# Hybrid encoder layer on one core: which engine makes the rest of an fp32r split for two weight units and four blocks of the down projection, an unrounded input summed instead of copied, and other banks for the keys' transposes

## Chip, cores and metric

The kernel runs on one core of a Trainium2 chip. The metric is the device time in microseconds (us) of one execution. A core has a matrix engine (TensorE, called PE in the profile), a vector engine (VectorE, DVE), a scalar engine (ScalarE, ACT), GpSimd (POOL) and a queue engine that starts DMAs (SyncE, SP). Every engine works through its own instructions in order and waits on semaphores.

## What is computed

One layer of an encoder for 512 tokens of width 1024, in float32: token mixing by two groups of heads (8 query heads over 2 key heads with a rotary embedding, and 4 heads of a two-way gated recurrence), cross attention of 4 heads into 256 memory tokens, and a gated feed-forward part of width 2816 with a convolution of three taps along the tokens. Each part has an RMS norm ahead and one behind.

```
h = rmsnorm(x, pre_mix_g)
aq, ak, av, hq, hf_fwd, hf_bwd, hi, hg = split_columns(h @ w_in, IN_SPLITS)
att = axial_gqa_attention(rope(rmsnorm(aq)), rope(rmsnorm(ak)), av)
rec = hgrn2_group(hq, hf_fwd, hf_bwd, hi, hg, lb, hg_out_norm_g)
x = x + rmsnorm(concatenate([att, rec]) @ w_out, post_mix_g)
h, m = rmsnorm(x, pre_x_g), rmsnorm(mem, mem_norm_g)
x = x + rmsnorm(memory_cross_attention(h, m, w_xq, w_xkv, w_xo), post_x_g)
h = rmsnorm(x, pre_ffn_g)
x = x + rmsnorm(conv_ffn(h, w_up, conv_w, conv_b, w_down), post_ffn_g)
```

## The kernel before

**Arithmetic.** A float32 operand is held as two fp32r parts: a high part, which is the value rounded by ACT (the cast in `split`, L118, `nc.scalar.copy(hi, src)`), and a low part, which is the rest, `src - hi` by DVE (L119). A product is three matmuls, high by high, high by low, low by high (`mm3`, L243 to L245); TensorE sums them in a bank of PSUM. PSUM has four kinds of bank, b, s, c and o, two of each.

**Weights.** They come in units of 128x1024 (512 KB), loaded by SP's queue into a raw buffer. `issue` (L198) makes the two parts three units ahead of the use (AHEAD). For most units ACT casts and DVE subtracts. For the units in NEG_SCALAR ACT casts (L212), ACT writes the negative of the high part into the low part (L214), and a DMA of GpSimd's queue adds the weight from DRAM to it once more (L217, `accum_op=ALU.add`); for those in NEG_POOL GpSimd makes the negative (L216).

**Order.** A scheduler puts the instructions of each engine in order when the program is built, out of the order of the code, the buffers that are free and its own estimates; the chip then keeps to that order on each engine. The large activations share 16 buffers ("big" in the profile).

**Keys.** While the recurrence of the last head and the attention run, `attention_filler` projects the memory's keys: eight projections, each of 24 matmuls of 128x256 into a bank b (`proj_fm`), which `put_kx` splits out of the bank by ACT and DVE. After the second and the third of them (KEY_TURNS) `turn_k` transposes the rotated keys of the token blocks 0, 1 and 2, 3 on TensorE (L715, four transposes each) into a bank b as well, and ACT copies them out (L716). L607 is a matmul of the recurrence into a bank c, between them.

**Into the feed-forward part.** `between` and `turn_in` make its input: DVE scales a block of 128 rows, TensorE transposes it into two banks (L282), and `split` takes the high part (ACT) and the low part (DVE) out of each bank. A third reader, ACT at L289, copies the unrounded values of each bank into `fulls`, two buffers of 128x4x512; there are four row blocks with two banks each, so eight copies of 128x512.

**Up projection.** 22 steps i; in five of them (5, 8, 11, 14, 17) a pair of column blocks is made by Strassen's seven products (`strassen_pair`). These need four differences of parts of the input, which `sum_of_h` makes from `fulls` (L1080, a subtraction of 128x1024 by DVE, then a split), one after each of the four units of the steps i = 2 and 3. The convolution of each step is `conv` (L1039 to L1053).

**Down projection.** Seven products p in Strassen's manner, each over three groups g of feed-forward blocks; a product takes 22 half units of weight, and two row blocks b. `left_side(p, g)` (L1010) prepares the left operand of one product and group: it splits a difference or a part of an activation into `hi` and `lo`. `lay_ahead` does this three groups ahead; (0,0) comes at the step i = 20 and (0,1), (0,2) at the end of the up projection. For most (p, g) it is ACT and DVE. For those in NEG_GROUP ACT casts (L1022), GpSimd writes the negative into `lo` (L1023), and a DMA of GpSimd's queue adds the source to it, from SBUF to SBUF (L1024). At p = 3 DVE overwrites a side buffer with another difference (L1014).

Of the kernel before, what the change touches and what calls it, by code (L numbers as in the profile page):

```python
# [9 lines left out]
F32 = mybir.dt.float32  # L10
# [8 lines left out]
P = 128  # L19
D = 1024  # L20
T = 512
# [16 lines left out]
UP_PRODUCTS = ("w11", "w22", "t2", "w21", "t1", "t3", "t4")  # L38
LAY_AHEAD, LOAD_AHEAD = 3, 5
SIDES_AT = (18, 19)  # L40
NEG_GROUP = frozenset((p, 1) for p in (1, 2, 5, 6))
AHEAD = 3
HOLD_BLOCK = 4
TURN_STEP, MEM_TURN, UP_TURN = 0, (0, 4), (0, 2)
NEG_SCALAR = frozenset(range(7, 31))
NEG_POOL = frozenset(range(31, 42))
CORE_SHARE, ATT_LEAD = 53.0, 4.0
KEY_TURNS = {1: (0, 1), 2: (2, 3)}
# [38 lines left out]
def layer(tc, io, out):  # L87
    nc = tc.nc
# [16 lines left out]
    def bank(tag):  # L105
        return ps.tile([P, 512], F32, name="ps_" + tag, tag=tag)

    def big(shape, dt=F32):
        return b8.tile(shape, dt, name="big", tag="big")
# [137 lines left out]
    def blk(b):  # L247
        return slice(b * P, (b + 1) * P)
# [26 lines left out]
        nc.vector.scalar_tensor_tensor(out=h[:, half(c)], in0=xb[:, half(c)], scalar=r, in1=g[:, half(c)],  # L275
                                       op0=ALU.mult, op1=ALU.mult)

    def turn_in(h, act, b, tags, keep=None):
        for c in range(2):
            o = bank(tags[c]).rearrange("p (k n) -> p k n", k=4)  # L280
            for k in range(4):
                nc.tensor.transpose(o[:, k, :], h[:, blk(c * 4 + k)], ident)  # L282
            hi, lo = act.hi, act.lo
            if len(hi) == 2:
                split(hi[c][:, :, blk(b)], lo[c][:, :, blk(b)], o)
            else:
                split(hi[0][:, c * 4:c * 4 + 4, blk(b)], lo[0][:, c * 4:c * 4 + 4, blk(b)], o)
            if keep:
                nc.scalar.copy(keep[c][:, :, blk(b)], o)  # L289

    def row_rstd(xb, h):
        ss = small()
# [13 lines left out]
        nc.vector.scalar_tensor_tensor(out=xb[:, cols], in0=yg, scalar=ss[:, R:R + 1], in1=xb[:, cols],  # L306
                                       op0=ALU.mult, op1=ALU.add)

    def between(x, g_post, g_pre, act, keep=None):
        def first(b, y):  # L310
            ss = small()
            return ss, residual_part(ss, y, g_post, 0, half(0), False, "th")

        def second(b, got, y):
            h = tmp4([P, D])
            ss = small()
            got = got[0], (got[1], residual_part(got[0], y, g_post, 1, half(1), True))
            for c in range(2):
                residual_add(got[0], got[1][c], x[b])
                nc.scalar.activation(h[:, half(c)], x[b][:, half(c)], ACT.Square, accum_out=ss[:, c:c + 1])  # L320
                rstd_part(ss, c, c == 1)
            for c in range(2):
                scale_rows(x[b], ss[:, R:R + 1], g_pre, h, c)
            return lambda: turn_in(h, act, b, y_tags[0][b] + y_tags[1][b], keep)
        return first, second

    def new_act():
# [37 lines left out]
    y_tags = ("b", "b", "c", "c"), ("s", "s", "o", "o")  # L365
# [68 lines left out]
    hT = new_act()  # L434
# [274 lines left out]
                                in1=kd[:, :, 0].bitcast(F32), op=ALU.subtract)  # L709

    def turn_k(b):
        o = bank("b").rearrange("p (k n) -> p k n", k=4)
        kd4 = qkv["kd"][:, b].rearrange("p a b c d -> p (a b) (c d)")
        for i in range(4):
            nc.tensor.transpose(o[:, i, :].bitcast(F32R), kd4[:, i, :], ident_r)  # L715
        nc.scalar.copy(qkv["kT"][:, :, blk(b)], o)  # L716
# [27 lines left out]
    tm_tags = ("s", "s", "o", "o")  # L744

    kv = {}
# [157 lines left out]
    x = load_x()  # L904
    g_post, g_pre = gains("post_mix_g", "pre_x_g")
    hT = new_act()

    turns = res_second(mix, MIX_ORDER, kv["y0"], between(x, g_post, g_pre, hT))
# [5 lines left out]
    qx, ox = Act([None] * 4, [None] * 4), Act([None] * 4, [None] * 4)  # L914
# [65 lines left out]

    g_post, g_pre = gains("post_x_g", "pre_ffn_g")
    hT = new_act()
    fulls = [big([P, 4, T]) for _ in range(2)]
    turns = res_second(ox, range(4), kv["x0"], between(x, g_post, g_pre, hT, fulls))

    acts, sides, gates, last_act = [], [], {}, [None]
    half_t = [slice(0, 256), slice(256, 512)]
# [75 lines left out]
    for part in range(2):  # L1063
        cols = slice(part * 256, part * 256 + 256)
        for n in range(4):
            for kc in range(8):
                mm3(us[n][:, cols], (ws[n][0][:, kc, :], ws[n][1][:, kc, :]), hT.get(kc, cols), kc == 0, kc == 7)
            if part:
                conv(*first[n], us[n])
            elif n in UP_TURN:  # L1070
                turns.popleft()()
    wide = [big([P, 2, 4, 256]) for _ in range(2)]
    s1, s2, s3, s4 = wide[0][:, 0], wide[0][:, 1], wide[1][:, 0], wide[1][:, 1]
    (a11, a21), (a12, a22) = [[f[:, :, t] for t in half_t] for f in fulls]
    sums_of_h = [(t[:, 0], t[:, 1]) for t in (big([P, 2, 4, 256], F32R) for _ in range(4))]
    of_h = [(s1, a21, a22), (s2, a11, s1), (s3, a21, a11), (s4, a12, s2)]

    def sum_of_h(k):
        o, i0, i1 = of_h[k]
        nc.vector.tensor_sub(o, i0, i1)  # L1080
        split(*sums_of_h[k], o)
# [43 lines left out]
    for i in range(2, NF):  # L1125
        if i in UP_S:
            strassen_pair(i)
        else:
            for c in range(2):
                o = next_bank()  # L1130
                w = unit(8)
                for kc in range(8):
                    mm3(o, (w[0][:, kc, :], w[1][:, kc, :]), hT.get(kc, slice(0, T)), kc == 0, kc == 7)
                conv(c, i, o)
                if i < 4:
                    sum_of_h(2 * i - 4 + c)
        if i % 3 == 2 and i // 3 < 6:
            new_sums(i // 3)

# [173 lines left out]
```

## Time and profile before

| | us |
|---|---|
| median of 3 runs | 825.16 (824.77 to 825.99) |
| the profiled execution | 825.72 |
| its span, first to last instruction | 823.8 |
| TensorE busy | 808.1 (98%) |
| VectorE busy | 568.5 (69%) |
| ScalarE busy | 473.0 (57%) |
| GpSimd busy | 132.3 (16%) |
| mean granted clock of TensorE | 0.999 of full |

The profile page gives busy times and groups of instructions by the code's line. The list of waits names, for an engine, the line that waited, the engine and line it waited for, and the time in total, the times, and the longest. The timeline gives each instruction's start and duration, and in brackets the idle time ahead of it with what ended that. A TensorE matmul's duration overlaps with the next one's, so the pitch of matmuls is read from start to start.

### The profile page before, as it was taken

What the parts mean: (1) busy time and instruction counts of PE and PEld (TensorE: products, weight loads), DVE (VectorE), ACT (ScalarE), POOL (GpSimd) and SP (SyncE); (2) the same over time, 40 slices, a digit from 0 to 9 for tenths busy, and PEclk for the clock granted to TensorE, in tenths of its full rate; (3) what the DMA queues carried; (4) which work ended last, traced back from release to release, by engine and by line L of the source; (5) the groups of instructions that cost most, each with busy time, mean ns of one, the idle gap of its engine ahead of it and who ended that gap; (6) DMA issues with size and microseconds to landing.
All of it is one profiled execution on the core that took longest, in us unless ns stands there. A gap on an engine that the chain in (4) does not pass through costs nothing.

```text
span 823.8 us, 11495 instructions
## 1 busy us (share of the span) xinstructions
PE 808.1 (98%) x4354; PEld 690.6 (84%) x4354; DVE 568.5 (69%) x849; ACT 473.0 (57%) x785; POOL 132.3 (16%) x194
## 2 busy tenths in 40 slices
PE   9999999999999999999999999999999999999996
PEld 7878888889898887888888898889889888878884
DVE  5347486569886875855453769787687796868865
ACT  6666756369788874645543665444344453556651
POOL 0110211044233101300001300111110102100302
PEclk9999999999999999999999999999999999999999
DMA  9696753657668533252212145787898885368842
GB/s 316 186 283 134 173 112 95 129 140 162 160 155 191 116 136 120 77 179 78 88 43 101 37 163 153 205 232 202 224 279 217 232 250 146 103 200 295 249 124 102
DMA packets 39671, 135.66 MB, mean 165 GB/s; under 512 B 5120, under 2 KB 6656, under 8 KB 39424
## 3 DMA queue, kind: packets, MB, share of 16 engines
q1 hardware_dynamic: 25632, 86.03, 30.0%
q0 software_dynamic: 10960, 40.38, 25.5%
q10 hardware_dynamic: 3024, 8.53, 2.9%
q8 instruction: 34, 0.56, 0.3%
q14 instruction: 21, 0.17, 0.1%
HBM read 130.72 MB, written 25.17 MB: 189 GB/s over the span
## 4 chain that ended last, share of the span: by engine, by line
PE 84%; DMA 4%; DVE 4%; issue 3%; ACT 2%; POOL 2%; SPq 0%; POOLq 0%; DVEq 0%; ACTq 0%
PE ps_b L243 9%; PE ps_b L244 9%; PE ps_b L245 9%; PE ps_s L244 6%; PE ps_s L245 6%; PE ps_s L243 6%; PE ps_o L243 5%; PE ps_o L245 5%; PE ps_o L244 5%; PE ps_c L245 4%; PE ps_c L244 4%; PE ps_c L243 4%; PE ps_c L607 3%; PE ps_o L851 2%; PE ps_s L830 2%
## 5 line engine op out<-in xcount | busy, mean ns | idle before, releaser
L119 DVE TENSOR_TENSOR wl<-raw,wh 128x1024 fp32r<-128x1024 f32 (+1 forms) x75 | 90.7, 1212 | 64.1 <-ACT wh L118 63.8
L118 ACT CAST wh<-raw 128x1024 fp32r<-128x1024 f32 (+1 forms) x75 | 76.8, 1027 | 83.0 <-PE ps_b L244 25.7
L243 PE MATMUL ps_b<-big,wh 128*128 128x512 f32 (+1 forms) x340 | 122.4, 360 | 0.7 <-DVE big L119 0.7
L245 PE MATMUL ps_b<-big,wl 128*128 128x512 f32 (+1 forms) x340 | 120.5, 355 | 0.0
L244 PE MATMUL ps_b<-big,wh 128*128 128x512 f32 (+1 forms) x340 | 120.5, 354 | 0.0
L243 PEld LDWEIGHTS ps_b<-big,wh 128*128 128x128 f32 x340 | 64.3, 189 | 9.2 <-DVE big L119 0.9
L244 PEld LDWEIGHTS ps_b<-big,wh 128*128 128x128 f32 x340 | 64.3, 189 | 8.6
L245 PEld LDWEIGHTS ps_b<-big,wl 128*128 128x128 f32 x340 | 64.2, 189 | 8.7
L633 DVE TENSOR_TENSOR big<-big 128x512 f32<-128x512 f32 x64 | 48.4, 761 | 16.4 <-PE ps_c L607 10.1
L244 PE MATMUL ps_s<-wl,big 128*128 128x512 f32 (+1 forms) x140 | 53.4, 381 | 2.6 <-DVE wl L119 1.7
L243 PE MATMUL ps_s<-wh,big 128*128 128x512 f32 (+1 forms) x140 | 53.5, 384 | 0.4 <-DVE big L119 0.4
L245 PE MATMUL ps_s<-wh,big 128*128 128x512 f32 (+1 forms) x140 | 53.1, 379 | 0.0
L212 ACT CAST wh<-raw 128x1024 fp32r<-128x1024 f32 x35 | 36.8, 1052 | 26.7 <-PE ps_b L244 12.9
L217 POOL DMA_DIRECT2D wl<-in_w_dram x35 | 30.9, 883 | 120.1 <-ACT wl L214 105.1
L119 DVE TENSOR_TENSOR big<-ps_o,big 128x512 fp32r<-128x512 f32 x54 | 37.0, 688 | 14.1 <-ACT big L118 12.2
L998 POOL DMA_DIRECT2D sum_t<-in_wd_dram x24 | 19.7, 833 | 143.7 <-DMA sum_t<-in_wd_dram 86.8
L118 ACT CAST big<-ps_o 128x512 fp32r<-128x512 f32 x54 | 31.6, 589 | 17.2 <-PE ps_o L953 7.5
L243 PE MATMUL ps_o<-wh,big 128*128 128x512 f32 (+1 forms) x102 | 39.3, 386 | 0.0
L244 PE MATMUL ps_o<-wl,big 128*128 128x512 f32 (+1 forms) x102 | 38.2, 375 | 0.0
L245 PE MATMUL ps_o<-wh,big 128*128 128x512 f32 (+1 forms) x102 | 38.2, 374 | 0.0
L244 PE MATMUL ps_c<-big,wh 128*128 128x256 f32 (+1 forms) x112 | 37.6, 336 | 0.0
L243 PE MATMUL ps_c<-big,wh 128*128 128x256 f32 (+1 forms) x112 | 37.6, 336 | 0.0
(311 smaller groups left out, 2171.0 us busy)
## 6 DMA issues: line engine op xcount, KB each, us to landing
raw<-in_w_dram SPq DMA_DIRECT2D x85, 512.0 KB, 3.3
wl<-in_w_dram POOLq DMA_DIRECT2D x35, 512.0 KB, 5.4
sum_t<-in_wd_dram POOLq DMA_DIRECT2D x20, 512.0 KB, 8.1
tmp<-in_w_dram SPq DMA_DIRECT2D x14, 512.0 KB, 6.0
sum_t<-in_wd_dram ACTq DMA_DIRECT2D x10, 512.0 KB, 6.2
sum_t<-sum_t POOLq DMA_DIRECT2D x10, 512.0 KB, 5.2
big<-sum_t SPq DMA_DIRECT2D x10, 512.0 KB, 4.9
raw<-sum_t SPq DMA_DIRECT2D x10, 512.0 KB, 4.5
```

The costliest lines, as they stand in the source:

```text
L118: nc.scalar.copy(hi, src)
L119: (eng or nc.vector).tensor_sub(lo, src, hi.bitcast(F32))
L212: nc.scalar.copy(wh, raw)
L217: nc.gpsimd.dma_start(wl, io["w"][i], accum_op=ALU.add)
L243: nc.tensor.matmul(o, a[0], b[0], start=start, stop=False, skip_group_check=again)
L244: nc.tensor.matmul(o, a[0], b[1], start=False, stop=False, skip_group_check=again)
L245: last_mm[0] = nc.tensor.matmul(o, a[1], b[0], start=False, stop=stop, skip_group_check=again).ins
L607: nc.tensor.matmul(o[:, b, :], kc[:, blk(b)], pat(qk, b * P, [[2 * m, P // (2 * m)], [T + m, 2], [1, m]]), start=True, stop=True)
L633: nc.vector.tensor_tensor(out=c, in0=c, in1=pat(tt, toff + off, [[2, npair], [gap, 2], [0, m]]), op=ALU.mult)
L830: nc.tensor.matmul(s, qT[h // 4][:, h % 4, blk(qb)], kT[:, 2 * (h // 4) + c, :], start=c == 0, stop=c == 1)
L851: nc.tensor.matmul(o, vv[:, c, h // 4].rearrange("p a d -> p (a d)"), pt[j][:, c, :], start=c + j == 0, stop=c == 3 and j == 1)
L998: nc.gpsimd.dma_start(t, weight_block(second_name, width(u)), accum_op=ALU.add)
```

## The change

Four edits. The low parts of weight units 7 and 8 are made by DVE and no longer by ACT and a DMA. In the down projection the group (0, 1) takes the way over GpSimd and its DMA, and (1, 1) that of ACT and DVE; before it was the other way round. The copies of the unrounded input at L289 are gone, and `full_h` adds the high and the low part back together by DVE, two additions of 128x2048 in step i = 2; all four `sum_of_h` follow in step i = 3, two after each unit. And `turn_k` takes its bank from `tm_tags[b]`, the bank kinds s, s, o, o in which the keys of the four blocks had been projected.

```
-NEG_GROUP = frozenset((p, 1) for p in (1, 2, 5, 6))
+NEG_GROUP = frozenset((p, 1) for p in (0, 2, 5, 6))
-NEG_SCALAR = frozenset(range(7, 31))
+NEG_SCALAR = frozenset(range(9, 31))
...
     def turn_in(h, act, b, tags):
...
-            if keep:
-                nc.scalar.copy(keep[c][:, :, blk(b)], o)
...
     def turn_k(b):
-        o = bank("b").rearrange("p (k n) -> p k n", k=4)
+        o = bank(tm_tags[b]).rearrange("p (k n) -> p k n", k=4)
...
-    fulls = [big([P, 4, T]) for _ in range(2)]
-    turns = res_second(ox, range(4), kv["x0"], between(x, g_post, g_pre, hT, fulls))
+    turns = res_second(ox, range(4), kv["x0"], between(x, g_post, g_pre, hT))
...
+    fulls = [big([P, 4, T]) for _ in range(2)]
     wide = [big([P, 2, 4, 256]) for _ in range(2)]
...
+    def full_h(k):
+        nc.vector.tensor_add(fulls[k], hT.hi[k].bitcast(F32), hT.lo[k].bitcast(F32))
...
-                if i < 4:
-                    sum_of_h(2 * i - 4 + c)
+                if i == 2:
+                    full_h(c)
+                elif i == 3:
+                    sum_of_h(2 * c)
+                    sum_of_h(2 * c + 1)
```

The `fulls` are now allocated behind the first loop over the units of the up projection. Lines move by 2 from L289 on and by 3 from L983 on: L715 becomes L713, L607 becomes L605, L1022 to L1024 become L1019 to L1021.

TensorE at the start of the down projection, product p = 0, the end of group 0 and the first matmuls of group 1 for the row block b = 0 (`big_6538` before and `big_6530` after are the left operand of (0, 1); `ps_b_6553` and `ps_b_6546` are the bank of b = 1). Before:

```order
L243 MATMUL ps_b_6552<-wh_6468,big_6464 128x512
L244 MATMUL ps_b_6552<-wl_6469,big_6464 128x512
L245 MATMUL ps_b_6552<-wh_6468,big_6464 128x512
L243 MATMUL ps_b_6552<-wh_6503,big_6538 128x512 [waits Activation_49]
L244 MATMUL ps_b_6552<-wl_6504,big_6538 128x512 [waits DVE_49]
L245 MATMUL ps_b_6552<-wh_6503,big_6538 128x512 [waits DVE_49]
L243 MATMUL ps_b_6552<-wh_6503,big_6538 128x512
L244 MATMUL ps_b_6552<-wl_6504,big_6538 128x512
L243 MATMUL ps_b_6553<-wh_6429,big_6464 128x512 [waits DVE_49,Activation_49]
```

And of the changed kernel:

```order
L243 MATMUL ps_b_6545<-wh_6460,big_6456 128x512
L244 MATMUL ps_b_6545<-wl_6461,big_6456 128x512
L245 MATMUL ps_b_6545<-wh_6460,big_6456 128x512
L243 MATMUL ps_b_6545<-wh_6495,big_6530 128x512 [waits Activation_49]
L244 MATMUL ps_b_6545<-wl_6496,big_6530 128x512 [waits DVE_49]
L245 MATMUL ps_b_6545<-wh_6495,big_6530 128x512 [waits DMASW3_49]
L243 MATMUL ps_b_6545<-wh_6495,big_6530 128x512
L244 MATMUL ps_b_6545<-wl_6496,big_6530 128x512
L243 MATMUL ps_b_6546<-wh_6421,big_6456 128x512 [waits DVE_49,Activation_49]
```

The order is the same; the matmul that first reads the low part of (0, 1) waited for DVE and now waits for a DMA of GpSimd's queue (DMASW).

TensorE at the transposes of the keys of the blocks 0 and 1, between the second and the third projection of the memory's keys. Before (`ps_b_1943` and `ps_b_1949` take the transposes, `ps_b_1955` is the third projection's bank):

```order
L245 MATMUL ps_b_1898<-big_1117,wl_1670 128x256
L715 MATMUL ps_b_1943<-ident_r_267,big_1755 128x128 [waits DVE_49]
L715 MATMUL ps_b_1943<-ident_r_267,big_1755 128x128 x3
L607 MATMUL ps_c_1934<-big_1406,tmp2_1932 128x128 [waits DVE_49,Activation_49]
L607 MATMUL ps_c_1934<-big_1406,tmp2_1932 128x128 x3
L715 MATMUL ps_b_1949<-ident_r_267,big_1755 128x128 [waits Activation_49]
L715 MATMUL ps_b_1949<-ident_r_267,big_1755 128x128 x3
L243 MATMUL ps_b_1955<-big_1117,wh_1724 128x256 [waits DVE_49]
L244 MATMUL ps_b_1955<-big_1118,wh_1724 128x256
L245 MATMUL ps_b_1955<-big_1117,wl_1725 128x256 [waits DMASW5_49]
```

And of the changed kernel, where `ps_s_1941` and `ps_s_1947` take the transposes:

```order
L245 MATMUL ps_b_1896<-big_1115,wl_1668 128x256
L713 MATMUL ps_s_1941<-ident_r_267,big_1753 128x128 [waits Activation_49]
L713 MATMUL ps_s_1941<-ident_r_267,big_1753 128x128 [waits DVE_49]
L713 MATMUL ps_s_1941<-ident_r_267,big_1753 128x128 x2
L713 MATMUL ps_s_1947<-ident_r_267,big_1753 128x128 [waits Activation_49]
L713 MATMUL ps_s_1947<-ident_r_267,big_1753 128x128 [waits DVE_49]
L605 MATMUL ps_c_1932<-big_1404,tmp2_1930 128x128 [waits DVE_49]
L605 MATMUL ps_c_1932<-big_1404,tmp2_1930 128x128 x3
L713 MATMUL ps_s_1947<-ident_r_267,big_1753 128x128 x2
L243 MATMUL ps_b_1953<-big_1115,wh_1722 128x256
L244 MATMUL ps_b_1953<-big_1116,wh_1722 128x256
L245 MATMUL ps_b_1953<-big_1115,wl_1723 128x256 [waits DMASW3_49]
```

The second block's transposes no longer wait for a copy out of the first one's bank, the recurrence's matmuls (L607, now L605) stand within them, and the third projection's first matmul has no wait left.

DVE in the steps i = 2 and 3 of the up projection: the first of the differences before, and the additions that stand there now, each with the rows up to the first difference (`big_4697` before and `big_4687` now take it). Before:

```order
L119 TENSOR_TENSOR wl_4705<-raw_4443,wh_4704 128x1024 [waits DMAHW5_49,PE_49,Activation_49]
L1040 SCALAR_TENSOR_TENSOR tmp2_4692<-ps_o_4450,cw_302,tmp2_4692 128x511 [waits Activation_49]
L1042 SCALAR_TENSOR_TENSOR tmp2_4692<-ps_o_4450,cw_302,tmp2_4692 128x511 [waits DVE_49]
L1053 TENSOR_TENSOR big_4637<-tmp2_4663,tmp2_4692 128x512 [waits DVE_49,Activation_49]
L1080 TENSOR_TENSOR big_4697<-big_4177,big_4178 128x1024
L188 TENSOR_TENSOR both_4837<-raw_4747,raw_4798 128x1024 [waits DMAHW7_49,DMAHW6_49]
L1040 SCALAR_TENSOR_TENSOR tmp2_4734<-ps_b_4703,cw_302,tmp2_4734 128x511 [waits Activation_49]
```

And of the changed kernel:

```order
L119 TENSOR_TENSOR wl_4695<-raw_4435,wh_4694 128x1024 [waits DMAHW5_49,PE_49,Activation_49]
L1037 SCALAR_TENSOR_TENSOR tmp2_4680<-ps_o_4442,cw_302,tmp2_4680 128x511 [waits Activation_49]
L1039 SCALAR_TENSOR_TENSOR tmp2_4680<-ps_o_4442,cw_302,tmp2_4680 128x511 [waits DVE_49]
L1050 TENSOR_TENSOR big_4625<-tmp2_4651,tmp2_4680 128x512 [waits DVE_49,Activation_49]
L1077 TENSOR_TENSOR big_4685<-big_4171,big_4173 128x2048
L1037 SCALAR_TENSOR_TENSOR tmp2_4724<-ps_b_4693,cw_302,tmp2_4724 128x511 [waits Activation_49]
L119 TENSOR_TENSOR wl_4732<-tmp4_4437,wh_4731 128x1024 [waits DMAHW0_49,PE_49]
L1039 SCALAR_TENSOR_TENSOR tmp2_4724<-ps_b_4693,cw_302,tmp2_4724 128x511 [waits DVE_49]
L1077 TENSOR_TENSOR big_4686<-big_4172,big_4174 128x2048
L188 TENSOR_TENSOR both_4826<-raw_4735,raw_4784 128x1024 [waits DMAHW7_49,DMAHW6_49]
L1037 SCALAR_TENSOR_TENSOR tmp2_4761<-ps_s_4730,cw_302,tmp2_4761 128x511 [waits Activation_49]
L1081 TENSOR_TENSOR big_4687<-big_4685,big_4686 128x1024 [waits DVE_49]
```

The two additions stand ahead of the first difference and behind the convolution of step 1; the four differences come later, close together.

More of the change, by code (lines that the diff above doesn't have):

```diff
@@ L276, in scale_rows, with turn_in @@
                                        op0=ALU.mult, op1=ALU.mult)
-    def turn_in(h, act, b, tags, keep=None):
+    def turn_in(h, act, b, tags):
         for c in range(2):
@@ L307, in residual_add, with between @@
                                        op0=ALU.mult, op1=ALU.add)
-    def between(x, g_post, g_pre, act, keep=None):
+    def between(x, g_post, g_pre, act):
         def first(b, y):
@@ L323, in second @@
                 scale_rows(x[b], ss[:, R:R + 1], g_pre, h, c)
-            return lambda: turn_in(h, act, b, y_tags[0][b] + y_tags[1][b], keep)
+            return lambda: turn_in(h, act, b, y_tags[0][b] + y_tags[1][b])
         return first, second
```

## The prediction

> **What bounds the kernel now.** I read the page first, for the engine that bounds. Its first lines:
>
> ```profile
> span 823.8 us, 11495 instructions
> PE 808.1 (98%) x4354; PEld 690.6 (84%) x4354; DVE 568.5 (69%) x849; ACT 473.0 (57%) x785; POOL 132.3 (16%) x194
> ```
>
> TensorE is busy 808.1 us of 823.8. No edit takes a matmul away, so the change can only touch the 15.7 us in which TensorE is idle, or add to them. The list of TensorE's waits tells what those are (columns: line that waits, line waited for, us in total, times, longest):
>
> ```profile
> PE ps_s L244 <- DVE wl L119: 1.7, 1, 1.7
> PE ps_b L432 <- DVE tmp L413: 1.3, 1, 1.3
> PE ps_s L244 <- DMA wl<-in_w_dram: 1.0, 1, 1.0
> PE ps_b L243 <- DVE big L119: 0.7, 1, 0.7
> PE ps_b L715 <- ACT big L716: 0.7, 2, 0.5
> ```
>
> Each edit aims at one of these or puts itself in front of one. Since a matmul's modelled end runs into the next one, idle time understates a stall; I count from start to start against the pitch of a row's neighbours. The profiled execution took 825.72 us, 1.92 more than its span and 0.56 above the median 825.16; the sum is made on 825.72 and carried to the median at the end. A measurement of this kernel can tell about 0.2% (1.65 us) from no change.
>
> **Units 7 and 8 by VectorE (a).** TensorE's timeline, and the chain of waits ahead of the second row:
>
> ```profile
> 50.14 0.39 PE L243 MATMUL ps_s<-wh,big 128*128 128x512 f32 x1
> 51.52 0.50 PE L244 MATMUL ps_s<-wl,big 128*128 128x512 f32 x1 [0.98 <-DMA wl<-in_w_dram]
> ```
>
> ```profile
> 43.06 8.41 DMA wl<-in_w_dram
> ```
>
> From 50.14 to 51.52 is one pitch, 0.23, and took 1.38; the matmul after the wait also takes 0.50 in place of 0.39. So 1.26 is lost, to a low part that landed 8.41 us after its DMA was issued. In its place DVE subtracts once per unit. The page has that form, and the window shows room on DVE:
>
> ```profile
> L119 DVE TENSOR_TENSOR wl<-raw,wh 128x1024 fp32r<-128x1024 f32 (+1 forms) x75 | 90.7, 1212 | 64.1 <-ACT wh L118 63.8
> ```
>
> ```profile
> 30.00:51.00 21.00, 20.53 (x95) 16.81 (x93) 7.66 (x15) 17.84 (x24) 2.79 (x3) 1.00 0.73 205
> ```
>
> DVE is busy 7.66 of 21 us there (third pair of busy time and count), so two subtractions of 1.21 hide, and the low part, begun at 43.06 at the latest, is ready by 44.3 where it is wanted at 50.4. The wait is the only one of its kind in the list, so the units behind, still by DMA, have slack. Gain 1.3; bounds 0.9 (the two units' ACT work moves, other work comes late by a little) and 1.3. If DVE had no room it would cost up to 2.4.
>
> **Keys' transposes (b).** TensorE's timeline from 206.40 on:
>
> ```profile
> 206.40 0.45 PE L715 MATMUL ps_b<-ident_r,big 128*128 128x128 f32 x4
> 207.22 1.20 PE L607 MATMUL ps_c<-big,tmp 128*128 128x128 f32 x8 [0.37 <-DVE tmp L697]
> 208.64 0.54 PE L715 MATMUL ps_b<-ident_r,big 128*128 128x128 f32 x4 [0.22 <-ACT big L716]
> 209.93 0.39 PE L243 MATMUL ps_b<-big,wh 128*128 128x256 f32 x1 [0.75 <-DVE big L119]
> ```
>
> Before, two banks b pass between transposes and projections, and each waits until ACT or DVE has emptied the one before last. By the order of the changed kernel the transposes go to banks s and o, and the third projection's first matmul waits for nothing. What stays is the recurrence's L607, which DVE releases at about 207.1. With eight of those (0.9 of pitch) and four transposes (0.3) behind it, the projection can start at about 208.4 where it starts at 209.93: 1.5. At the second pair the longer of the two waits for L716 in the list, 0.5, goes as well. Gain 2.0; at least 1.3 (0.75 in brackets and that 0.5), at most 2.3 (if the lag of a start behind each of these releases, some 0.15 twice, goes too). Next in line is the first softmax of the attention, whose length doesn't change while no less TensorE work than before stands between its scores and its transposes; if that cover were short, up to 1 us of the gain would go.
>
> **The copies (c).** TensorE and DVE at the last block's transposes:
>
> ```profile
> 478.30 0.28 PE L245 MATMUL ps_c<-big,wl 128*128 128x256 f32 x1
> 479.06 0.66 PE L282 MATMUL ps_c<-ident,tmp 128*128 128x128 f32 x4 [0.48 <-ACT big L289]
> 479.55 0.60 PE L282 MATMUL ps_o<-ident,tmp 128*128 128x128 f32 x4
> 480.79 0.39 PE L243 MATMUL ps_o<-big,wh 128*128 128x256 f32 x1 [0.64 <-ACT big L289]
> ```
>
> ```profile
> 479.43 0.69 DVE L119 TENSOR_TENSOR big<-ps_o,big 128x512 fp32r<-128x512 f32 x1
> ```
>
> A pitch behind 478.30 the transposes could start at 478.42, and they start 0.64 later. The next matmul into a bank o starts at 480.79, once the copy that stands behind the two parts of the split has left the bank. Without the copy the bank is free when DVE's part ends: at 480.12, or 0.2 sooner since ACT's queue is shorter. So the matmul starts at about 479.95: gain 0.85. Bounds 0.6 (only its bracketed wait) and 1.4 (nothing but TensorE's own work from 478.42). The other four of the eight copies are waited for by nobody.
>
> **The sum instead (d).** DVE's last split of a difference, and TensorE's first matmul that reads that:
>
> ```profile
> 519.93 1.22 DVE L119 TENSOR_TENSOR big<-big 128x1024 fp32r<-128x1024 f32 x1
> ```
>
> ```profile
> 529.38 0.28 PE L243 MATMUL ps_b<-big,wh 128*128 128x256 f32 x1
> ```
>
> An addition of 128x2048 isn't in the trace; twice this one of 128x1024 gives 2.4, so the two cost DVE about 4.9 us. DVE's last split ends at 521.15, then at about 526; it is needed at 529.38. Cost nothing, with some 3.4 us of cover; if that were gone, the overshoot would be paid in full, up to about 1.5.
>
> **The group of the down projection (e).** Before, at (1, 1). The chain of waits and TensorE there, then DVE:
>
> ```profile
> 716.50 1.05 ACT big L1022
> 717.64 1.95 POOL big L1023
> 719.88 8.46 DMA big<-big
> ```
>
> ```profile
> 729.60 0.39 PE L243 MATMUL ps_s<-wh,big 128*128 128x512 f32 x1
> 731.64 0.50 PE L244 MATMUL ps_s<-wl,big 128*128 128x512 f32 x1 [1.66 <-DVE wl L119]
> ```
>
> ```profile
> 728.36 1.23 DVE L1014 TENSOR_TENSOR big<-big 128x1024 f32<-128x1024 f32 x1 [4.83 <-DMA big<-big]
> ```
>
> DVE may not overwrite the side at L1014 before that DMA has read it. It stands 4.83 us, the low part of a weight queues behind it, and TensorE loses 2.04 less a pitch of 0.23 and again 0.1 in the matmul after the wait, that is 1.9. With (1, 1) by ACT and DVE this goes; the subtraction comes in place of (0, 1)'s, so DVE has no more to do.
>
> But (0, 1) takes that way now, and it is wanted early. ACT's first cast of a left side of this stage, and TensorE's matmul that reads the low part of (0, 1), the fifteenth of the stage:
>
> ```profile
> 706.34 1.79 ACT L118 CAST big<-big 128x1024 fp32r<-128x1024 f32 x2 [0.99 <-PE ps_b L244]
> ```
>
> ```profile
> 712.26 0.39 PE L245 MATMUL ps_b<-wh,big 128*128 128x512 f32 x1
> ```
>
> The cast waits for a buffer that TensorE frees with the last unit of the up projection, so it can't come sooner. What follows is the chain above, with the spread of its four cases (ns) and landings (us):
>
> ```profile
> L1023 POOL TENSOR_SCALAR big<-big x4: 1043/1322/1941, 717.6 to 777.9; 128x1024 fp32r<-128x1024 f32 x4
> ```
>
> ```profile
> DMA to landing us min/median/max: 7.1/8.4/11.3
> ```
>
> 706.34 + 1.05 (cast) + 0.1 + 1.3 (GpSimd) + 0.3 + 8.4 (DMA) = 717.5, the two small terms being the gaps in the chain between 717.55 and 717.64 and between 719.59 and 719.88. TensorE reaches 712.26 and stands until then, for 5.2, with 0.1 for the slow first matmul: 5.3. Nothing can go past it: the order has the two other matmuls of row block 0 behind it and then row block 1, on the same queue. With the shortest parts (1.04 and 7.1) the stall is 3.7, with the longest (1.94 and 11.3) 8.8. Net of the 1.9: +3.4, bounds +1.8 and +6.9.
>
> A page's figure for the DMA: the Trainium skill, "DMA: Bandwidth & Descriptors", section "Anatomy of one DMA — SWDGE (gpsimd) path", fits 2.0 us + bytes/436e3 per DMA, an estimate of 3.2 us for these 512 KB. By it the part would land at 712.3, there would be no stall, and the sum would be 6.1 us lower than before; the four landings here took 7.1 to 11.3, so the measurement decides. It is the far end of the first rival below.
>
> **The sum.** -1.3 - 2.0 - 0.85 + 0 + 3.4 = -0.75. On the profiled execution that is 824.97, on the median 825.16 it is 824.4.
>
> **The rivals.** All on the median.
>
> *The DMA lands early.* The DMA of (0, 1) could land like those of the weights' low parts. The page's row for these gives the median:
>
> ```profile
> wl<-in_w_dram POOLq DMA_DIRECT2D x35, 512.0 KB, 5.4
> ```
>
> With 5.4 in place of 8.4 the stall is 2.3, (e) nets +0.4 and the sum is -3.75: 821.4. Against it: those come from DRAM, and all four from SBUF to SBUF took 7.1 or more. For it: four are a small sample, and the stage ahead of (0, 1) is another one than theirs.
>
> *The clock falls (the other side).* TensorE's windows at the end of the run (its busy time and count, and, behind the five engines, its granted clock), and its first rows:
>
> ```profile
> 816.00:821.00 5.00, 0.41 (x2) 0.00 (x0) 2.40 (x5) 0.95 (x4) 1.07 (x3) 1.00 0.29 111
> 821.00:822.00 1.00, 0.00 (x0) 0.00 (x0) 0.00 (x0) 0.00 (x0) 0.00 (x0) 0.88 1.03 370
> 822.00:823.00 1.00, 0.00 (x0) 0.00 (x0) 0.00 (x0) 0.00 (x0) 0.00 (x0) 0.50 0.01 3
> ```
>
> ```profile
> 1.26 3.75 PE L432 MATMUL ps_b<-tmp,ones 128*128 128x256 f32 x8 [1.26 <-DVE tmp L413]
> 5.19 0.79 PE L471 MATMUL ps_s<-wh,big 128*128 128x512 f32 x1 [0.17 <-ACT wh L447]
> 5.78 0.48 PE L471 MATMUL ps_o<-wh,big 128*128 128x512 f32 x1
> ```
>
> The last matmul ends at about 816.4. A mean of 0.88 over the sixth us is half speed in its last 0.24, so the clock fell at 821.76, 5.35 after the end of work. No gap inside the kernel reaches 2 us now; the new one has 5.3, just at that edge. If the clock falls within it, the matmuls behind run at half pitch until it is back. At the start TensorE works from 1.26 and takes 0.59 for a pitch still at 5.19, so it is slow for some 4 to 4.6 us, half of which is lost: +2.0, estimated 1.7 to 2.3. The sum is then +1.25: 826.4, slower. It decides once the stall passes the time that the clock holds, which lies between the longest bracketed wait of today, 1.7, and 5.35. The Trainium skill, "TensorE: Matmul & The Clock Gate", section "What's actually happening", has the clock fall to half after one idle window of about 3.4 us, and the windows run free of the kernel. By that rule a gap of 5.3 would be enough in about half of the runs; the 5.35 here is within what the rule allows.
>
> *The DMA lands like the slowest.* With 11.3 the stall is 8.2, net +6.3, the sum +2.2, and at such a gap, past 5.35, the clock falls too, +2.0: 829.3. For it: one of the four landings was that slow. Against it: the other three were not above 8.5, since the median is 8.4 and the one in the chain 8.46.
>
> *The banks bring nothing (b at 0.5) or the additions come late.* If the attention's first softmax takes the time back, or DVE's 5 us reach TensorE's 529.38, the sum is +0.8: 826.0.
>
> **How the numbers follow.** My forecast 0.40; early landing 0.23; clock 0.21; slowest landing 0.09; banks or additions 0.07. The forecast's own range is 822.3 (b, c and the landing at their ends in favour) to 825.8 (a, b and c at the others). The range of 821.0 to 827.0 takes in all but the slowest landing and the edges. Faster by over 0.2% (below 823.5): the early landing 0.23 and a quarter of the forecast, 0.10: 0.33. Slower (above 826.8): the slowest landing 0.09, half of the clock's case, 0.10, and 0.03 of the last one: 0.22. Within 0.2%: the rest, 0.45.
>
> **What would show it.** In the trace of the changed kernel: no wait of L244 on a DMA near 50; no wait of the transposes at L713 and of the matmul behind them; the last transposes' matmul at L243 released by DVE L119; no wait near 525 to 537; no wait near 728; and one wait of L245 for a DMA into `big` near 708, of 4 to 6 us, with the clock at 1.00 behind it. The forecast is wrong if that stall is under 3 or over 7 us, if the clock falls behind it, or if a new wait stands where one went.

## The result, and the profile after

The changed kernel took 831.38 us (median of 5 runs, 828.14 to 832.81) against 825.16 (824.77 to 825.99). The medians differ by 6.2; the ratio, taken over all runs, is 1.0068 with a 95% interval of 1.0045 to 1.0092, so 5.6 us slower (3.7 to 7.6). The forecast of 824.4 was wrong, and its range of 821.0 to 827.0 does not hold the time. One execution of the kernel with both repairs (1345.89 us, the one that was profiled) and one of a kernel with unread matmuls (2880.28) ran far outside all others and stand in no ratio or spread below. The profiled execution of the changed kernel took 830.35 us, 4.63 more than that of before. Its page:

```profile
span 828.2 us, 11485 instructions
PE 808.9 (98%) x4354; PEld 691.5 (83%) x4354; DVE 573.4 (69%) x853; ACT 466.8 (56%) x775; POOL 128.5 (16%) x192
```

TensorE has as many matmuls as before and is busy as long; the span has grown by idle time, and a little by slow matmuls. The list of TensorE's waits:

```profile
PE ps_b L245 <- DMA big<-big: 6.2, 1, 6.2
PE ps_c L605 <- ACT tmp L602: 2.4, 1, 2.4
PE ps_b L430 <- DVE tmp L411: 1.3, 1, 1.3
PE ps_s L469 <- ACT wh L445: 0.9, 2, 0.5
PE ps_c L605 <- DVE big L631: 0.6, 2, 0.4
```

All that the edits aimed at is gone: no wait of L244 on DVE or on a weight's DMA, none of the transposes (now L713), none of L282 or behind it. Two waits are new, 6.2 and 2.4 us. The first is the one that the prediction forecast near 708; it stands at 710. TensorE's timeline:

```profile
710.11 0.39 PE L244 MATMUL ps_b<-wl,big 128*128 128x512 f32 x1
716.65 0.79 PE L245 MATMUL ps_b<-wh,big 128*128 128x512 f32 x1 [6.15 <-DMA big<-big]
717.24 0.63 PE L243 MATMUL ps_b<-wh,big 128*128 128x512 f32 x1
717.67 0.63 PE L244 MATMUL ps_b<-wl,big 128*128 128x512 f32 x1
...
721.08 0.43 PE L244 MATMUL ps_b<-wl,big 128*128 128x512 f32 x1
721.35 0.40 PE L245 MATMUL ps_b<-wh,big 128*128 128x512 f32 x1
```

From 710.11 to 716.65 TensorE lost 6.54 less a pitch of 0.23, that is 6.3. Behind it the rows take 0.63 for 0.39 and stand 0.43 apart, until 721.08: ten matmuls in 4.43 us for 2.27, so another 2.2. The windows of that stretch give the clock (the figure ahead of the last two):

```profile
711.00:714.00 3.00, 0.00 (x0) 0.00 (x0) 2.93 (x4) 0.00 (x0) 0.00 (x0) 1.00 0.90 219
714.00:715.00 1.00, 0.00 (x0) 0.00 (x0) 0.48 (x1) 0.00 (x0) 0.00 (x0) 0.67 1.23 198
715.00:721.00 6.00, 4.35 (x10) 3.47 (x11) 0.00 (x0) 0.11 (x1) 0.00 (x0) 0.50 0.15 23
721.00:722.00 1.00, 1.00 (x5) 0.79 (x4) 0.02 (x1) 0.94 (x1) 0.00 (x0) 0.92 0.00 0
```

A mean of 0.67 is half speed in the last two thirds of that us: the clock fell at about 714.3, 3.8 us after the end of the last matmul, and 0.92 in the last row puts its return at about 721.2, 4.5 us after work had begun again. The chain of waits ahead of the stall has its sizes:

```profile
705.57 1.07 POOL big L1020
706.64 0.29 issue
706.92 9.68 DMA big<-big
```

The second new wait was not forecast. TensorE and ACT near 60:

```profile
60.27 0.39 PE L245 MATMUL ps_s<-wh,big 128*128 128x512 f32 x1
63.01 1.16 PE L605 MATMUL ps_c<-big,tmp 128*128 128x128 f32 x8 [2.35 <-ACT tmp L602]
```

```profile
56.73 1.08 ACT L214 ACTIVATE wl<-wh 128x1024 fp32r<-128x1024 f32 x1
61.76 0.69 ACT L669 ACTIVATE big<-big,rx 128x128 f32<-128x128 f32 x2 [3.96 <-DMA big<-in_rope_dram]
62.36 0.60 ACT L602 COPY tmp<-big 128x512 f32<-128x512 f32 x1
```

L669 scales the rotary tables (`rope_tables`), which nobody needs for long. It waits 3.96 us for their load, and L602, a copy that the recurrence's next matmuls read, stands behind it on ACT. In the kernel before the scaling stood two copies further back. ACT's order, before and then after:

```
L604 COPY tmp2_510<-big_322 128x512 [waits DVE_49]
L214 ACTIVATE wl_530<-wh_529 128x1024 [waits DMASW0_49,Activation_49]
L212 CAST wh_593<-raw_591 128x1024 [waits DMAHW2_49]
L604 COPY tmp2_540<-big_322 128x512 [waits DVE_49]
L214 ACTIVATE wl_594<-wh_593 128x1024 [waits DMASW1_49,Activation_49]
L604 COPY tmp2_557<-big_322 128x512 [waits DVE_49]
L671 ACTIVATE big_458<-big_458,rx_281 128x2x64 [waits DMAHW1_49]
```

```
L602 COPY tmp2_508<-big_322 128x512 [waits DVE_49]
L214 ACTIVATE wl_528<-wh_527 128x1024 [waits Activation_49]
L669 ACTIVATE big_456<-big_456,rx_281 128x2x64 [waits DMAHW1_49]
L669 ACTIVATE big_456<-big_456,rx_281 128x2x64
L602 COPY tmp2_538<-big_322 128x512 [waits DVE_49]
```

The load itself is no slower than it was. Its DMA in the trace of before, then in that of after (min, median and max of one):

```profile
L720 ACTq DMA_DIRECT2D big<-in_rope_dram x1: 495/495/495, 47.6 to 47.6; - x1
DMA to landing us min/median/max: 15.3/15.3/15.3
```

```profile
L718 ACTq DMA_DIRECT2D big<-in_rope_dram x1: 677/677/677, 47.7 to 47.7; - x1
DMA to landing us min/median/max: 14.1/14.1/14.1
```

So before it landed at 62.9, and its reader came at 64.32 (`64.32 1.28 ACT L671` in ACT's timeline); after, it landed at 61.8 and its reader had been ready at 57.8.

The other two edits did what they should. TensorE at the keys' transposes, and at the last block's transposes into the feed-forward part:

```profile
208.07 0.63 PE L713 MATMUL ps_s<-ident_r,big 128*128 128x128 f32 x6
208.81 1.23 PE L605 MATMUL ps_c<-big,tmp 128*128 128x128 f32 x8
209.78 0.38 PE L713 MATMUL ps_s<-ident_r,big 128*128 128x128 f32 x2
```

```profile
477.92 0.60 PE L282 MATMUL ps_c<-ident,tmp 128*128 128x128 f32 x4
478.35 0.60 PE L282 MATMUL ps_o<-ident,tmp 128*128 128x128 f32 x4
478.90 0.36 PE L243 MATMUL ps_o<-big,wh 128*128 128x256 f32 x1
```

No bracket is left in them. The matmul at L243 that stood at 480.79 starts 0.55 behind the transposes ahead of it; it stood 1.24 behind them.

### The profile page after: what moved, and what is told of

Same layout as the page of the kernel before. It is cut to its first block, busy times and chain, and to the rows that moved or that the text cites. A ratio compares the mean times of both kernels' runs of the same rounds, so it can differ in the third digit from the quotient of the medians.

```text
span 828.2 us, 11485 instructions
## 1 busy us (share of the span) xinstructions
PE 808.9 (98%) x4354; PEld 691.5 (83%) x4354; DVE 573.4 (69%) x853; ACT 466.8 (56%) x775; POOL 128.5 (16%) x192
## 4 chain that ended last, share of the span: by engine, by line
PE 91%; DMA 4%; DVE 2%; ACT 1%; POOL 0%; issue 0%; SPq 0%; POOLq 0%; ACTq 0%; DVEq 0%
PE ps_b L245 10%; PE ps_b L244 9%; PE ps_b L243 9%; PE ps_s L244 6%; PE ps_s L243 6%; PE ps_s L245 6%; PE ps_o L243 5%; PE ps_o L244 5%; PE ps_o L245 5%; PE ps_c L243 4%; PE ps_c L244 4%; PE ps_c L245 4%; PE ps_c L605 3%; PE ps_o L849 2%; PE ps_s L828 2%; DMA big<-in_rope_dram 2%
## 5 line engine op out<-in xcount | busy, mean ns | idle before, releaser
L118 ACT CAST wh<-raw 128x1024 fp32r<-128x1024 f32 (+1 forms) x77 | 78.9, 1028 | 93.5 <-PE ps_b L244 22.0
L243 PE MATMUL ps_b<-big,wh 128*128 128x512 f32 (+1 forms) x340 | 122.4, 360 | 0.0
L244 PE MATMUL ps_b<-big,wh 128*128 128x512 f32 (+1 forms) x340 | 120.4, 354 | 0.0
L244 PEld LDWEIGHTS ps_b<-big,wh 128*128 128x128 f32 x340 | 64.3, 189 | 8.4
L243 PEld LDWEIGHTS ps_b<-big,wh 128*128 128x128 f32 x340 | 64.3, 189 | 8.3
L243 PE MATMUL ps_s<-wh,big 128*128 128x512 f32 (+1 forms) x140 | 53.3, 382 | 0.4 <-DVE big L119 0.4
L244 PE MATMUL ps_s<-wl,big 128*128 128x512 f32 (+1 forms) x140 | 53.1, 379 | 0.0
L212 ACT CAST wh<-raw 128x1024 fp32r<-128x1024 f32 x33 | 34.7, 1052 | 24.2 <-PE ps_b L244 12.9
L217 POOL DMA_DIRECT2D wl<-in_w_dram x33 | 29.1, 881 | 124.1 <-ACT wl L214 103.8
L245 PE MATMUL ps_b<-wh,big 128*128 128x512 f32 x92 | 36.7, 401 | 6.2 <-DMA big<-big 6.2
L243 PE MATMUL ps_o<-wh,big 128*128 128x512 f32 (+1 forms) x102 | 39.5, 387 | 0.0
L244 PE MATMUL ps_o<-wl,big 128*128 128x512 f32 (+1 forms) x102 | 38.4, 376 | 0.0
L243 PE MATMUL ps_b<-wh,big 128*128 128x512 f32 x92 | 38.1, 415 | 0.0
```

The lines of the kernel that those rows point to most:

```text
L212: nc.scalar.copy(wh, raw)
L217: nc.gpsimd.dma_start(wl, io["w"][i], accum_op=ALU.add)
L243: nc.tensor.matmul(o, a[0], b[0], start=start, stop=False, skip_group_check=again)
L244: nc.tensor.matmul(o, a[0], b[1], start=False, stop=False, skip_group_check=again)
L245: last_mm[0] = nc.tensor.matmul(o, a[1], b[0], start=False, stop=stop, skip_group_check=again).ins
```

## The experiments

Theory A: the loss is the group (0, 1), by a stall of 6.3 us and the clock that falls in it, 2.2, less the old stall's 1.9. Theory B: it lies in the first stages, where ACT's order has changed. The two traces give room to both, A more than B. All times are medians; the ratio is to the kernel before on the same chip and taken over all runs, so it compares kernels that ran on different chips better than the medians do. The kernel before took 825.57 beside the first four, 824.99 beside the next four and 825.02 beside the last four.

### The group put back

```
-NEG_GROUP = frozenset((p, 1) for p in (0, 2, 5, 6))
+NEG_GROUP = frozenset((p, 1) for p in (1, 2, 5, 6))
```

> The changed kernel with the group of the down projection put back, (1, 1) over GpSimd and its DMA, (0, 1) by ACT and DVE; the other three edits stay. Theory A (the group costs: a stall of 6.3 us at the start of the down projection, 2.0 by the clock that falls in it, less the 1.9 of the old stall): about 6.4 us less than the changed kernel's 831.4, so 825.0. Theory B (the loss sits in the first stages, where ACT now waits for a load; the down projection only shows it): within 1 us of 831.4. If A holds, the trace still shows the recurrence's wait of 2.3 us near 60.

824.29 us (821.26 to 827.35, 12 runs), ratio 0.9986 (0.9971 to 1.0). TensorE's waits:

```profile
PE ps_c L605 <- ACT tmp L602: 2.4, 1, 2.4
PE ps_s L244 <- DVE wl L119: 1.5, 1, 1.5
```

Theory A holds for the larger part: without the group the other three edits are 1.2 us faster than the kernel before (0 to 2.4). The old wait behind L1014 is back, and the recurrence's wait is still there.

### Units 7 and 8 alone

```
-NEG_SCALAR = frozenset(range(7, 31))
+NEG_SCALAR = frozenset(range(9, 31))
```

> The kernel before with one edit, units 7 and 8 by DVE. Theory A says nothing of it; by the prediction on record it gains 1.3: 823.9. Theory B (ACT's scaling of the rope tables moves ahead of two copies of the recurrence, and waits there for its load): the stall of 1.3 near 50 goes and one of 2.4 near 60 comes, net +1.2: 826.3.

827.2 us (825.25 to 830.02, 12 runs), ratio 1.0021 (1.001 to 1.0033): 1.7 slower. The list of waits has the new one in place of the old:

```profile
PE ps_c L607 <- ACT tmp L604: 2.2, 1, 2.2
```

Theory B holds as well, as a second and smaller loss: this edit, which the prediction had at a gain, costs.

### The group alone

```
-NEG_GROUP = frozenset((p, 1) for p in (1, 2, 5, 6))
+NEG_GROUP = frozenset((p, 1) for p in (0, 2, 5, 6))
```

> The kernel before with one edit, the group (0, 1) in place of (1, 1). Theory A: +6.4 on 825.2, so 831.6, with a wait of 6 us or more near 712 and the clock under 1 behind it. Theory B: within 1 us of before. By the prediction on record +3.4: 828.6.

832.15 us (830.74 to 834.2, 6 runs), ratio 1.0081 (1.0064 to 1.0097): 6.7 slower, with TensorE's wait and the slow row behind it as in the changed kernel:

```profile
710.68 0.39 PE L244 MATMUL ps_b<-wl,big 128*128 128x512 f32 x1
717.07 0.79 PE L245 MATMUL ps_b<-wh,big 128*128 128x512 f32 x1 [6.00 <-DMA big<-big]
717.66 0.63 PE L243 MATMUL ps_b<-wh,big 128*128 128x512 f32 x1
```

### TensorE kept busy in the stall

The row block 1 of the first four half units is put behind the wait by hand, nearly as the order has it anyway, and unread matmuls stand ahead of the wait:

```
+        if (p, b) == (0, 1) and j < 4:
+            late.append((j, w))
+            return
+        if (p, j, b) == (0, 4, 0):
+            nc.tensor.matmul(y[b], hi[ac], w[0][:, wc], start=False, stop=False)
+            nc.tensor.matmul(y[b], hi[ac], w[1][:, wc], start=False, stop=False)
+            idle = bank("c")
+            for _ in range(KEEP):
+                one = nc.tensor.matmul(idle, hi[ac], w[0][:, wc], start=True, stop=True).ins
+            with tc.issue_after(one):
+                nc.tensor.matmul(y[b], lo[ac], w[0][:, wc], start=False, stop=False)
...
```

> The changed kernel with 23 matmuls of 128x512 (5.2 us) that nobody reads put into TensorE's order right ahead of the matmul that waits for the DMA of (0, 1); the useful order behind is the same, and the wait shrinks to about 1 us, since the DMA lands when it did. If the clock's fall is part of the loss, the time is about 2.0 under the changed kernel's 831.4, so 829.4, with the clock at 1.00 behind the stall. If the wait alone is the loss, it stays at 831.4 or a little above.

827.26 us (825.21 to 831.38, 12 runs), ratio 1.0029 (1.0013 to 1.0045): 4.1 under the changed kernel by the medians and 3.2 by the ratios, where 2.0 was expected. The trace tells why the comparison is not clean. The clock does stay at 1.00 there, but the load of the rotary tables landed after 11.9 us in this execution and not after 14.1, ACT stood 1.84 us for it, and TensorE's wait near 60 is not in the list. So the load's landing, which differs from run to run, is in the spread of each kernel with this order, and the clock had to be measured without it (below).

### The rotary tables loaded first

```
-        mem_load()
-        load_tables()
+        load_tables()
+        mem_load()
```

> The changed kernel with the load of the rope tables started ahead of the three loads of the memory on ACT's queue, and nothing else. If ACT's wait for that load is what holds the recurrence near 60, the wait of 2.3 us goes: 829.0 for 831.4. If ACT's new order itself holds it (the scaling standing ahead of the copies), little changes: within 0.7 of 831.4.

827.36 us (826.85 to 828.76, 10 runs), ratio 1.0028 (1.0019 to 1.0038): 4.0 under the changed kernel by the medians and 3.3 by the ratios, where 2.4 was expected. The load is issued at 41.9 and no longer queues behind three loads of 512 KB:

```profile
DMA to landing us min/median/max: 3.9/3.9/3.9
```

The scaling (L669) still stands ahead of the copies on ACT, but it starts at 57.35 and waits for nothing, so it was the load that held the recurrence there and not the new order alone. TensorE's wait near 60 is gone and the spread is 1.9 us, where the group put back, with the wait, has 6.1.

What goes beyond 2.4 is within the spread of the changed kernel's five runs, and it has a cause that another trace shows (below, at GpSimd's subtraction): in some executions the clock falls behind this wait too, which costs another 1.5 us. The mean clocks fit that. With the group put back, six of twelve runs have 0.997 to 0.999 and 821.26 to 823.6 us, the other six 0.993 to 0.996 and 824.98 to 827.35. Of the changed kernel's five runs the profiled one, whose clock stayed at 1.00 near 60, has 0.993, and three have 0.991 and 831.38 to 832.81 us. That the clock fell at this wait in those runs is inferred; they were not traced.

### Neither group over GpSimd

```
-NEG_GROUP = frozenset((p, 1) for p in (0, 2, 5, 6))
+NEG_GROUP = frozenset((p, 1) for p in (2, 5, 6))
```

> The changed kernel with neither (0, 1) nor (1, 1) over GpSimd; (2, 1), (5, 1) and (6, 1) stay. By theory A both stalls of the down projection go: the old one of 1.7 too, which the kernel with (1, 1) put back still shows. 822.5. If DVE, which makes one more low part, gets late somewhere, 824 or more.

820.74 us (819.56 to 821.57, 6 runs), ratio 0.9942 (0.9929 to 0.9954). Its first waits show what is left of the change's cost, here a little shorter:

```profile
PE ps_c L605 <- ACT tmp L602: 1.7, 1, 1.7
PE ps_b L430 <- DVE tmp L411: 1.3, 1, 1.3
```

DVE makes both low parts and nothing waits for it. The mean clock is 0.997 or 0.998 in all six runs.

### Both repairs

The last two edits together.

> The changed kernel with both repairs, the rope tables loaded first and neither (0, 1) nor (1, 1) over GpSimd. If the two losses are separate they add: 831.4 - 2.4 - 8.9 = 820.1, and no wait of TensorE over 0.6 us is left behind its start. If they share a cause, it is no better than the better of the two alone, about 822.5.

819.22 us (818.61 to 819.36 in five runs), ratio 0.9923 (0.9911 to 0.9935), 6.4 us faster than the kernel before (5.4 to 7.3), and the fastest of all. It is 1.5 under the better of the two repairs, so the two losses are separate. What the repairs gain singly by the medians, 4.0 and 10.6, is more than the 12.2 of both: without the groups the wait near 60 was only 1.7 and no run has a low clock, so there was less for the tables to gain. No line of a profile of this kernel is read here.

### GpSimd subtracts, without a DMA

```
+            if p == 0:
+                nc.gpsimd.tensor_sub(lo, src, hi.bitcast(F32))
+            else:
...
```

> The changed kernel, but GpSimd subtracts for (0, 1) itself and no DMA follows; the rest of that way stays. If the DMA's 9.7 us are the cause of the stall, the low part is ready some 2 to 3 us after the cast, ahead of TensorE, and the time is 831.4 - 8.4 = 823.0. If GpSimd as such is too slow there, a stall of its own length stays, and the time is over 825.

823.06 us (819.17 to 823.87, 9 runs), ratio 0.9967 (0.9953 to 0.9981). GpSimd's one row in place of a row and a DMA:

```profile
706.64 2.40 POOL L1021 TENSOR_TENSOR big<-big 128x1024 fp32r<-128x1024 f32 x1 [6.70 <-ACT big L1019]
```

It ends at 709.04. TensorE's matmul that reads it, the fifteenth of the stage, starts at 711.42 and doesn't wait for it. The 9.7 us of the DMA were the stall; GpSimd was not.

The tables are loaded last here, as in the changed kernel, and in this execution the clock fell behind TensorE's wait for ACT near 60:

```profile
62.57 1.16 PE L605 MATMUL ps_c<-big,tmp 128*128 128x128 f32 x8 [2.28 <-ACT tmp L602]
...
63.82 0.63 PE L244 MATMUL ps_s<-wl,big 128*128 128x512 f32 x1
...
68.92 1.13 PE L605 MATMUL ps_c<-big,tmp 128*128 128x128 f32 x8
```

The granted clock is 0.78 in the half us from 63.50, 0.50 from 64.00 to 67.00 and 0.81 in the half us behind. So it fell at 63.8, when TensorE had been at work again for 1.2 us, and was down for 3.4 us. From the first of these rows to the last 6.35 us passed; the changed kernel's trace, with the clock at 1.00 there, has 4.80 for the same matmuls (63.01 to 67.81). The fall cost 1.55 us behind a wait of only 2.28. The waits of 2.35 in the changed kernel's trace and of 2.2 in that of units 7 and 8 alone had no such fall.

### The clock alone: the unread matmuls with the tables loaded first

> The kernel with the rope tables loaded first (827.4, and a narrow spread), with the 23 unread matmuls ahead of the wait as well. Here only the clock differs between the two: if its fall costs what the slow rows behind the stall show (nine or ten pitches of 0.43 for 0.23), the time is 2.0 less, 825.4. If the wait alone is the loss, 827.4.

825.21 us (824.74 to 825.70 in ten runs); ratio 1.0001 (0.9991 to 1.001). Against 827.36 that is 2.15 less (2.2 by the ratios), for the same wait: the clock's fall costs about 2.1 us. TensorE's rows:

```profile
707.39 5.38 PE L1170 MATMUL ps_c<-wh,big 128*128 128x512 f32 x23
713.60 0.50 PE L1172 MATMUL ps_b<-wh,big 128*128 128x512 f32 x1 [0.83 <-DMA big<-big]
713.94 0.40 PE L244 MATMUL ps_b<-wh,big 128*128 128x512 f32 x1
```

### Ten unread matmuls

`KEEP = 10` in place of 23.

> As the last one with 10 unread matmuls (2.3 us) for 23, so that a gap of about 4.0 us is left. In the changed kernel's trace the clock fell about 3.8 us after the last matmul, at the end of the run 5.35 us after it. If the time that the clock holds is fixed near 5.3, it stays at 1.00 and the time is 825.4; if it is fixed under 4, it falls each time and the time is 827.4; if it differs from run to run between these, most runs keep the clock and some lose up to 2 us.

828.07 us (826.68 to 828.49, 6 runs), ratio 1.0034 (1.0022 to 1.0045). All six lie above all ten of the last kernel, so the clock seems to have fallen in each. The trace has it for one:

```profile
714.01 0.79 PE L1172 MATMUL ps_b<-wh,big 128*128 128x512 f32 x1 [3.83 <-DMA big<-big]
```

```profile
713.00:714.00 1.00, 0.00 (x0) 0.00 (x0) 0.02 (x1) 0.00 (x0) 0.00 (x0) 0.78 0.22 34
714.00:717.00 3.00, 2.98 (x7) 2.41 (x8) 0.00 (x0) 0.00 (x0) 0.00 (x0) 0.50 0.00 0
```

0.78 is half speed from 713.56 on, 3.4 us after the end of the last unread matmul (707.75 + 2.43). A gap of 4.0 us was enough. That the median came out 0.7 above the kernel with the full gap fits the time for which the clock stayed down. In this trace it was back at 717.0, after 3.4 us; in the trace of the changed kernel it was down for 6.8, and over 2 us of that fell into the gap, where it costs nothing. Two of the six runs have a mean clock of 0.997 and took 826.68 (the profiled one) and 827.03 us; the other four have 0.993 or 0.994 and took 828.0 to 828.49, about 3 more than with 23 unread matmuls. About 3 is what 6.8 us at half speed cost when nearly all of them meet work, an estimate; these four runs were not traced.

### The banks alone

```
-        o = bank("b").rearrange("p (k n) -> p k n", k=4)
+        o = bank(tm_tags[b]).rearrange("p (k n) -> p k n", k=4)
```

> The kernel before with one edit, the keys' transposes in banks s and o. By the prediction on record 2.0 less, by the traces of the two kernels (start to start over that stage) 2.1 less: 823.0. If the time comes back later in the attention, no difference: 825.1.

822.77 us (821.3 to 823.98, 8 runs), ratio 0.9974 (0.9964 to 0.9985): 2.1 faster, as forecast; nothing comes back later.

### The sums alone

The changed kernel with its other three edits undone:

```
-NEG_GROUP = frozenset((p, 1) for p in (0, 2, 5, 6))
+NEG_GROUP = frozenset((p, 1) for p in (1, 2, 5, 6))
-NEG_SCALAR = frozenset(range(9, 31))
+NEG_SCALAR = frozenset(range(7, 31))
...
-        o = bank(tm_tags[b]).rearrange("p (k n) -> p k n", k=4)
+        o = bank("b").rearrange("p (k n) -> p k n", k=4)
```

> The kernel before with one edit, the copies of the unrounded input gone and DVE's sums in their place. By the prediction on record 0.85 less, by the two traces 1.45 less, since the matmul that waited for the last copy waits for nothing now: 823.7. If DVE's 5 us reach the first Strassen pair, 825.1 or more.

823.56 us (822.54 to 827.78, 12 runs), ratio 0.9986 (0.9973 to 0.9999): 1.2 faster. DVE's longer queue reaches nobody. The profiled execution took 825.86, and its trace shows 1.5 of the 2.3 us by which it lies above the median. At the keys' transposes, whose banks are the old ones in this kernel, TensorE waits three times, 0.38, 0.20 and 0.75 us; behind the third, at 210.4, the clock fell for 3.4 us, and 18 matmuls took 3.76 us that take 2.26 in the trace of the kernel before.

## Why the prediction was wrong, point by point

| term | forecast | the two traces | alone |
|---|---|---|---|
| units 7 and 8 | -1.3 | -1.3 + 2.5 | +1.7 (0.8 to 2.7) |
| banks | -2.0 | -2.1 | -2.1 (-3.0 to -1.2) |
| copies and sums | -0.85 | -1.45 | -1.2 (-2.2 to -0.1) |
| group | +3.4 | 6.3 + 2.2 - 1.9 = +6.6 | +6.7 (5.3 to 8.0) |
| sum | -0.75 | +4.3 | +5.1 |

The traces' 2.5 is the start-to-start loss between 60.27 and 63.01, and the 0.4 that is left of the 4.63 between the two profiled executions is about the start, where TensorE waited longer for its first weights (0.9 at L469). That units 7 and 8 alone cost 1.7 and not the 1.2 of the two traces fits the falls of the clock behind the new wait in some runs; no trace of that kernel shows one.

**Units 7 and 8: the step failed.** The prediction priced what the edit removes and adds and asked whether DVE had room. It did, and the stall near 50 went as forecast. It did not ask what else stands in another order because ACT has less to do. The scheduler moved the tables' scaling ahead of two copies, into the 15.3 us of a load whose reader had until then come just late enough. All of it was to be had before the run: ACT's order of the two kernels, the load's landing at 62.9 and its reader at 64.32 in the trace of before. "The wait is the only one of its kind in the list, so the units behind, still by DMA, have slack" looked for the next wait of the same kind, not for the next wait.

**The group: the mechanism was right, its size and its state were not.** The stall stood where it was forecast, on the matmul that was named. Of its parts the cast was as priced, 1.05, and GpSimd took 1.07 for 1.3; the DMA took 9.68 for the median's 8.4, and between 9.53 and 9.68 in each of the kernels above that have it. The median of four transfers at other moments was no estimate for this one, and the spread of 7.1 to 11.3 held it. What makes it 9.6 there was not tried. The clock's fall, which stood among the rivals with 0.21, came true with its price of 2.0 (measured 2.1). It should have been part of the forecast, and its condition was wrong: the prediction had the clock hold for one length of time, between 1.7 and 5.35 us, with the upper end from a single fall at the end of a run. The traces show no such time: the clock fell behind a wait of 2.28 us in one execution and stayed up behind 2.35 in another. The Trainium skill, "TensorE: Matmul & The Clock Gate", section "What's actually happening", has the clock fall after one idle window of about 3.4 us. The length agrees with the 3.4 us, and twice 3.4, for which the clock was down in these traces; that TensorE must be idle for so long does not, by the fall behind 2.28 us.

**Banks: right**, by the steps as put, and the attention's softmax didn't take it back.

**Copies: right in kind, too small.** The prediction took the bank's release from DVE's row at 479.43 and moved it by 0.2. With the copies gone from ACT's queue the whole chain of splits ahead moved up: DVE's row starts 0.27 behind TensorE's last matmul ahead of the transposes (478.07 behind 477.80), where it was 1.13. The matmul waits for nothing: the bound of 1.4 was the value.

**Sums: right.** Each addition took 2.28 us against the 2.4 assumed, and nothing waits between 525 and 537.

The rivals "lands early" and "slowest landing" did not happen. No forecast or rival held the recurrence's wait.

## What to carry to other kernels

Where a scheduler writes the order, an edit that takes work off an engine must be followed through that whole engine's new order, above all to each instruction that waits for a load: a load that takes 15 us and is read 1.4 us after it lands is a stall that only the old order kept away. An accumulating DMA that takes 9.5 to 9.7 us, as this one did in six traces, has no place in a chain that is wanted within 6; either the engine subtracts itself, here in 2.4 us, or the group is one with time. And a stall of TensorE must be priced with the slow matmuls that can stand behind it: here 2.1 us on top of 6.3, each time that was traced, and 1.55 on top of 2.28 in one execution of several. Where such a fall comes and goes, the runs of one kernel spread by it, and the mean clock of each run helps to tell them apart.

## What the runs showed of the hardware

- In the gaps of TensorE at the start of the down projection the clock fell 3.2 to 4.2 us after the end of the last matmul, in each of the four traces in which nothing or too little filled the gap (the changed kernel, the group alone, the tables first, ten unread matmuls). It stayed down for 6.8 us in the first three and for 3.4 in the last.
- It also fell, for 3.4 us, behind a single wait of 2.28 us and behind three waits of 1.33 us in all, and each of these falls cost about 1.5 us. The trace of the kernel before has the same three waits, and there it fell only at the end of the run, 5.35 us after the last matmul.
- In the changed kernel's trace the clock changed at 714.34, 721.16 and 823.56, at distances of 2 and 30 times 3.41 us. So the changes seem to lie on a grid of 3.41 us, and a wait's place on it could decide whether the clock falls behind it, which would explain why the same wait brings it down in one execution and not in another. No run tested that.
- 23 matmuls that nobody reads save 2.1 us in a wait that they don't shorten.
- A load of 256 KB took 11.9 to 15.7 us behind three loads of 512 KB on the same queue (ten traces), and 3.0 to 3.9 ahead of them (three). Where it is waited for, this difference is in the spread of the runs.
- GpSimd's subtraction of 128x1024 took 2.40 us, twice DVE's 1.22, and still beat its own way over the DMA, which takes 1.07 + 0.29 + 9.68, by 8.6 us.
